# A state space mixer's elementwise work: Horner steps, compact products and rotations placed on VectorE

## The chip, the cores and the metric

The kernel runs on one core of a Trainium2 chip as one program. The metric is the time of one execution in device microseconds (us). TensorE multiplies matrices into PSUM, VectorE (DVE in the profile) and GpSimd (POOL) do elementwise work, ScalarE (ACT) copies and applies functions, SyncE (SP) issues the DMA transfers. GpSimd instructions here read and write SBUF only; VectorE reads and writes SBUF and PSUM.

## The reference

Two transformer blocks run one after the other on 512 tokens of width 1024. Only the first block's state space mixer bears on the change. For 32 groups of 16 channels with 64 complex states each it discretises a diagonal system, runs it over the sequence and mixes the result:

```python
h = rmsnorm(x, norm1_g[l]); hp = h @ w_in[l]
y_ssm = s5_mixer(hp[..., :512], ...)
y_nsa = nsa_mixer(hp[..., 512:1024], ...)
gate = sigmoid(hp[..., o4:])                   # 2 x 1024 columns
merged = gate0 * (y_ssm @ w_proj_ssm) + gate1 * (y_nsa @ w_proj_nsa)

def s5_mixer(u, a_re, a_im, log_dt, b_re, b_im, c_re, c_im, d_skip, w_glu, b_glu):
    dt = exp(log_dt)[:, None]
    mag = exp(a_re * dt)
    abar_re, abar_im = mag * cos(a_im * dt), mag * sin(a_im * dt)
    fr, fi = ((abar - 1) / (a_re + i a_im))     # real and imaginary part
    bbar = f * b                                # complex, 64 states x 16 channels
    bu = einsum('bsgc,gpc->bsgp', ug, bbar)
    x = associative_scan(x_t = abar * x_{t-1} + bu_t)
    y = einsum(x_re, c_re) - einsum(x_im, c_im) + d_skip * ug
    yg = gelu(y)
    return yg * sigmoid(yg @ w_glu + b_glu)
```

## The kernel before

A planner orders the instructions of each engine ahead of time from their dependencies and their place in the program; the chip then runs each engine's list in that order. Every float32 matrix product is split into a high and a low part, so a weight tile of 128x1024 is loaded (`wload`, line 217: a DMA to `raw`, a ScalarE copy to `wh`, a VectorE subtraction to `wl`) and takes 24 matmuls of 512 columns (`mm3`, line 204). Two `raw` buffers and three of `wh` and `wl` exist. In PSUM there are four buffers of the kind `mm`, three of the kind `aux` and one of the kind `sm`.

The first stage runs to about 208 us. `block1` (line 425) loads the parameters and calls `s5_params` (line 469), which works out the exponentials, sines and cosines by polynomials on tiles of 128x16, all on GpSimd (tile `s5s`). `s5` (line 553) projects the mixer's input (4 units of `win`, evicted to `uv`, spread by DMA to `ur`), then runs `s5_half` twice, once for each half of the states, with `gates` (line 1113) after each: 8 projection units whose results VectorE scales (`gt`, tt on line 189) and ScalarE passes through the sigmoid. At the end `glu` (line 763) projects the mixer's output. Only when the tiles of this stage are free can the attention stage (`nsa_proj`) allocate its own; its first instruction on GpSimd is the memset of `hsel` on line 790.

Inside `s5_half` time is cut into chunks of four steps. `cm` (line 605) multiplies complex parameter columns into the matrices of 128x8x32 by three VectorE instructions of 256 elements each: 8 calls build `T1` (tiles `s5A`, `s5B`) for the four lags and 8 build `CA` (`s5CAr`, `s5CAi`). Half of each 32-column block is zero, since two groups share a block. `P` (`s5Pr`, `s5Pi`) holds 128 powers of a phase, doubled in seven levels of six GpSimd instructions each. TensorE transposes `T1` to `W1` (line 657), builds the direct term `KT` and `G` (lines 666 to 685), and for each of two `jt` computes `wr`, `wi` in PSUM (line 694). VectorE turns them by the phase (four multiplications), GpSimd adds (`s5C` or `glus`), VectorE scans with decay `m4` (line 717, eight scans of 128), four multiplications turn the result back, GpSimd adds into `s5Xr`, `s5Xi`, and TensorE sums `py` (lines 733 and 735). `self.tt` on line 189 takes the engine as its last argument, so nearly all of this stands on lines 189, 194 and 195 of the profile.

Of the kernel before, what the change touches and what calls it, by code (L numbers as in the profile page):

```python
# [7 lines left out]
F32 = mybir.dt.float32  # L8
# [4 lines left out]
OP = mybir.AluOpType  # L13
# [9 lines left out]
C1 = 6.28125  # L23
C2 = 0.0019350051879882812
# [28 lines left out]
def pack(a):  # L53
    f = {}
# [35 lines left out]
    f["s5b"] = np.stack([bd(a["ssm_b_re"][0]), bd(a["ssm_b_im"][0])], 1)  # L90
# [87 lines left out]
class Kern:  # L178
# [246 lines left out]
    def block1(self):  # L425
# [5 lines left out]
        with ExitStack() as st0:  # L431
            mg = self.pool(st0, "mg")
            self.mg = mg
            self.y_ssm = [mg.tile([128, 4, T], F32R, name="ys" + n) for n in "HL"]
            with ExitStack() as st1:
                p = self.pool(st1, "s5c")
                prm = p.tile([128, 3, 16], F32, name="s5p")
                nc.sync.dma_start(prm, I["s5p"])
                par = self.s5_params(p, prm)
                xp = self.pool(st1, "s5h")  # L440
                xs, pre = [], []
                for k in range(4):
# [5 lines left out]
                self.s5(xp, p, hs, par, xs, pre)  # L448
# [20 lines left out]
    def s5_params(self, p, prm):  # L469

        nc, I = self.nc, self.I
        e = nc.gpsimd
# [4 lines left out]
        def new():  # L477
            cnt[0] += 1
            return big[:, cnt[0] - 1]

        def tt(a, b, op):
            o = new()
            self.tt(o, a, b, op, e)
            return o

        def ts(a, s1, op0, s2=None, op1=None):
            o = new()
            self.ts(o, a, s1, op0, s2, op1, e)
            return o

        add, sub, mul = OP.add, OP.subtract, OP.mult

        def exp_parts(x):

            x = ts(x, -87.0, OP.max, 88.0, OP.min)
            n = ts(x, 1.0 / math.log(2.0), mul, MAGIC, add)
            n = ts(n, MAGIC, sub)
            r = tt(x, ts(n, LN2_HI, mul), sub)
            r = tt(r, ts(n, LN2_LO, mul), sub)
# [5 lines left out]
            self.ts(si, n, 127.0, add, 8388608.0, mul, e)  # L505
            return q, si.bitcast(F32)

        q, s = exp_parts(ldt)
        dt = tt(tt(s, q, mul), s, add)
        q, s = exp_parts(tt(ar, dt, mul))  # L510
        em = tt(tt(s, q, mul), ts(s, 1.0, sub), add)
# [3 lines left out]
        r = tt(th, ts(k, C1, mul), sub)  # L515
        r = tt(r, ts(k, C2, mul), sub)
        r = tt(r, ts(k, C3, mul), sub)
        h = ts(r, 0.5, mul)
        h2 = tt(h, h, mul)
        s = ts(h2, -1.0 / (12 * 13), mul, 1.0, add)  # L520
        for i in (10, 8, 6, 4, 2):
            s = ts(tt(s, h2, mul), -1.0 / (i * (i + 1)), mul, 1.0, add)
        s = tt(s, h, mul)
        c = ts(h2, -1.0 / (13 * 14), mul, 1.0, add)
        for i in (11, 9, 7, 5, 3, 1):
            c = ts(tt(c, h2, mul), -1.0 / (i * (i + 1)), mul, 1.0, add)
        cm1 = ts(tt(s, s, mul), -2.0, mul)
        sn = ts(tt(s, c, mul), 2.0, mul)
        cs = ts(cm1, 1.0, add)
        nr = tt(tt(em, cs, mul), cm1, add)  # L530
        mag = ts(em, 1.0, add)
        a1r, a1i = tt(mag, cs, mul), tt(mag, sn, mul)
        den = tt(tt(ar, ar, mul), tt(ai, ai, mul), add)
        rd = new()
        nc.vector.reciprocal(rd, den)
        fr = tt(tt(tt(nr, ar, mul), tt(a1i, ai, mul), add), rd, mul)
        fi = tt(tt(tt(a1i, ar, mul), tt(nr, ai, mul), sub), rd, mul)

        def cmul(x, y):
            return (tt(tt(x[0], y[0], mul), tt(x[1], y[1], mul), sub),  # L540
                    tt(tt(x[0], y[1], mul), tt(x[1], y[0], mul), add))

        A = [None, (a1r, a1i)]
        A.append(cmul(A[1], A[1]))
        A.append(cmul(A[2], A[1]))
        A.append(cmul(A[2], A[2]))
        m2 = tt(mag, mag, mul)
        m4 = tt(m2, m2, mul)
        u2 = cmul((cs, sn), (cs, sn))
        u4 = cmul(u2, u2)  # L550
        return A, (fr, fi), m4, u4

    def s5(self, hp, p, hs, par, xs, pre):
        nc, I = self.nc, self.I
        A, F, m4, u4 = par
# [20 lines left out]
        self.proj(I["win"][0:4], hs, u_out, first=3, pre=dict(enumerate(pre)), mid0=norm, mid_at=-3)  # L576
        for a in range(2):
# [3 lines left out]
        self.s5_half(hp, 0, A, F, m4, u4, s5d, ur, uv1)  # L581
        self.gates(hs, 0)
        self.s5_half(hp, 1, A, F, m4, u4, s5d, ur, uv1)
# [3 lines left out]
    def s5_half(self, hp, hf, A, F, m4, u4, s5d, ura, uv1):  # L587
        nc, I = self.nc, self.I
        add, sub, mul = OP.add, OP.subtract, OP.mult
        e, ep = nc.vector, nc.gpsimd  # L590
# [34 lines left out]

# [4 lines left out]
        self.ts(P[0][:, :, 1], u4[0][:, ps], 1.0, mul, e=ep)  # L630
        self.ts(P[1][:, :, 1], u4[1][:, ps], 1.0, mul, e=ep)
        n = 1
        while n < 128:

            m = min(n, 127 - n)
            if m > 0:
# [9 lines left out]
                self.tt(t, xi, sr, mul, ep)  # L646
                self.tt(oi, xr, si, mul, ep)
                self.tt(oi, oi, t, add, ep)
            n *= 2

# [36 lines left out]
        for jt in (2 * hf, 2 * hf + 1):  # L687
# [11 lines left out]
            ab, cd = (t2("s5A"), t2("s5B")) if jt % 2 == 0 else (t2("s5W1r"), t2("s5W1i"))  # L699
            ta, tb, tc, td = ab[:, 0], ab[:, 1], cd[:, 0], cd[:, 1]  # L700
            if jt % 2 == 0:
                zc = t2("s5C")
                zr, zi = zc[:, 0], zc[:, 1]
            else:
                zr, zi = (tile([128, 512], "glus", 2) for _ in range(2))
# [1352 lines left out]
```

## Time and profile before

| what | value |
|---|---|
| median of 3 runs | 1677.97 us (1674.24 to 1678.4) |
| profiled execution | 1677.89 us, its span 1676.2 us |
| TensorE / VectorE busy in the span | 94% / 69% |
| ScalarE / GpSimd busy in the span | 44% / 30% |

A page of the profile gives each engine's busy time, the chain of work that ended last, and groups of instructions by line, engine and tile. Views of the trace used here are the busy time by stretch, the waits of one engine, the groups with shapes kept apart, and instructions in order of time. A group's mean is the duration of one instruction; neighbours on an engine overlap by a little, so the distance between two starts is what one costs in a sequence.

### The profile page before, as it was taken

The page shows a single profiled execution, that of the slowest core. Times are in us where ns is not written, and L with a number is a line of the kernel's source. Part 1 is how long each engine was busy: PE and PEld are TensorE (multiplying, and loading weights), DVE is VectorE, ACT ScalarE, POOL GpSimd, SP SyncE. Part 2 cuts the span into 40 slices and gives each one's busy share as a digit, 9 for nine tenths or more (in the row PEclk, how much of TensorE's full clock was granted, in tenths as well). Part 3 has the DMA queues.
Part 4 walks back from the last instruction along what each step waited for, and adds up shares of the span by engine and source line. Part 5 has one row for each costly group of instructions (what it writes and reads, how often), then busy time and mean ns, then how long its engine had stood idle before and what let it go on. Part 6 is the DMA issues. An engine that isn't in the chain of part 4 may idle for free.

```text
span 1676.2 us, 22389 instructions
## 1 busy us (share of the span) xinstructions
PE 1574.8 (94%) x8277; PEld 1311.6 (78%) x8277; DVE 1156.2 (69%) x2075; ACT 731.4 (44%) x1284; POOL 506.8 (30%) x586
## 2 busy tenths in 40 slices
PE   7779998899999999999999999989989899999997
PEld 5567776677798888888887888878878788888886
DVE  5889644576759963864446878576877798767655
ACT  4214725454444322342235555466654444434332
POOL 7866122221300000000022222224420466555552
PEclk9898999799999999999999999999999899999998
DMA  4231241001436773743221111111221223323322
GB/s 171 69 91 40 92 127 38 7 21 50 139 138 204 227 262 99 237 153 100 89 70 51 39 40 43 58 58 63 62 64 56 76 91 98 101 89 100 101 79 85
DMA packets 59756, 158.34 MB, mean 94 GB/s; under 512 B 12416, under 2 KB 19840, under 8 KB 59520
## 3 DMA queue, kind: packets, MB, share of 16 engines
q1 hardware_dynamic: 59648, 156.92, 29.4%
q8 instruction: 65, 1.06, 0.3%
q14 instruction: 43, 0.35, 0.1%
HBM read 152.57 MB, written 2.10 MB: 92 GB/s over the span
## 4 chain that ended last, share of the span: by engine, by line
PE 71%; DVE 15%; issue 4%; POOL 4%; ACT 4%; DMA 1%; SPq 0%; POOLq 0%; DVEq 0%; ACTq 0%
PE ps_mm L208 20%; PE ps_mm L210 20%; PE ps_mm L209 20%; DVE wl L189 2%; PE ps_sm L1093 2%; PE ps_mm L1082 1%; DVE caccm L198 1%; POOL s5s L189 1%; ACT L186 1%; DVE s5t L189 1%; DVE hgE L189 1%; POOL s5s L195 1%; DVE s5CAr L189 1%; PE ps_aux L1536 1%; DVE s5CAi L189 1%
## 5 line engine op out<-in xcount | busy, mean ns | idle before, releaser
L186 ACT ACTIVATE wh<-raw 128x1024 fp32r<-128x1024 f32 (+3 forms) x234 | 236.6, 1013 | 549.0 <-PE ps_mm L209 408.7
L189 DVE TENSOR_TENSOR wl<-raw,wh 128x1024 fp32r<-128x1024 f32 (+2 forms) x162 | 197.9, 1222 | 119.7 <-ACT wh L186 110.4
L198 DVE SCALAR_TENSOR_TENSOR caccf<-ps_mm,cwf,caccf 128x441 f32<-128x441 f32 (+2 forms) x308 | 206.7, 694 | 34.6 <-ACT ctapf L186 28.9
L189 POOL TENSOR_TENSOR wl<-raw,wh 128x1024 fp32r<-128x1024 f32 (+2 forms) x72 | 159.9, 2222 | 167.4 <-ACT wh L186 166.7
L208 PE MATMUL ps_mm<-h4H,wh 128*128 128x512 f32 (+1 forms) x368 | 137.1, 380 | 7.8 <-DVE caccf L198 7.6
L189 POOL TENSOR_TENSOR rr<-rv,nhalf 128x2 f32<-128x2 f32 x9 | 8.7, 969 | 435.9 <-DVE rv L195 435.9
L210 PE MATMUL ps_mm<-h4H,wl 128*128 128x512 f32 (+1 forms) x368 | 138.3, 378 | 0.0
L209 PE MATMUL ps_mm<-h4L,wh 128*128 128x512 f32 (+1 forms) x368 | 138.3, 379 | 0.0
L208 PE MATMUL ps_mm<-h2H,wh 128*128 128x512 f32 (+1 forms) x280 | 103.8, 372 | 0.0
L210 PE MATMUL ps_mm<-h2H,wl 128*128 128x512 f32 (+1 forms) x280 | 103.6, 371 | 0.0
L209 PE MATMUL ps_mm<-h2L,wh 128*128 128x512 f32 (+1 forms) x280 | 103.6, 371 | 0.0
L208 PE MATMUL ps_mm<-aH,wh 128*128 128x512 f32 (+1 forms) x272 | 102.6, 377 | 0.5 <-DVE x L189 0.5
L210 PE MATMUL ps_mm<-aH,wl 128*128 128x512 f32 (+1 forms) x272 | 102.7, 378 | 0.0
L209 PE MATMUL ps_mm<-aL,wh 128*128 128x512 f32 (+1 forms) x272 | 102.4, 377 | 0.0
L208 PE MATMUL ps_mm<-hH,wh 128*128 128x512 f32 x224 | 89.7, 407 | 11.3 <-ACT hH L186 10.7
L210 PE MATMUL ps_mm<-hH,wl 128*128 128x512 f32 x224 | 90.5, 406 | 7.7 <-DVE wl L189 7.7
L1228 DVE CUSTOM_DVE_ANT_0 msc<-wmod,cB,cols 128x1024 bf16<-128x1024 f32 x64 | 82.0, 1281 | 20.5 <-DMA wmod<-in_wmod 20.2
L209 PE MATMUL ps_mm<-hL,wh 128*128 128x512 f32 x224 | 90.9, 406 | 0.0
L208 PEld LDWEIGHTS ps_mm<-h4H,wh 128*128 128x128 f32 x368 | 68.7, 190 | 21.2 <-issue 7.7
L209 PEld LDWEIGHTS ps_mm<-h4L,wh 128*128 128x128 f32 x368 | 69.9, 190 | 13.2 <-DVE h4L L198 0.4
L210 PEld LDWEIGHTS ps_mm<-h4H,wl 128*128 128x128 f32 x368 | 69.8, 190 | 13.1
L208 PE MATMUL ps_mm<-faH,wh 128*128 128x512 f32 (+1 forms) x194 | 72.4, 373 | 0.0
(531 smaller groups left out, 4141.7 us busy)
## 6 DMA issues: line engine op xcount, KB each, us to landing
raw<-in_wup SPq DMA_DIRECT2D x76, 512.0 KB, 3.5
wmod<-in_wmod SPq DMA_DIRECT2D x48, 512.0 KB, 4.3
raw<-in_wdn SPq DMA_DIRECT2D x32, 512.0 KB, 3.5
raw<-in_win SPq DMA_DIRECT2D x28, 512.0 KB, 3.5
raw<-in_wout SPq DMA_DIRECT2D x8, 512.0 KB, 3.5
raw<-in_wdn2a SPq DMA_DIRECT2D x8, 512.0 KB, 3.4
raw<-in_wdn2b SPq DMA_DIRECT2D x8, 512.0 KB, 3.3
raw<-in_wdn2c SPq DMA_DIRECT2D x8, 384.0 KB, 3.1
```

The lines of the kernel that those rows point to most:

```text
L186: return self.nc.scalar.activation(o, i, f, **k)
L189: return (e or self.nc.vector).tensor_tensor(o, a, b, op)
L195: return e.tensor_scalar(o, a, s1, s2, op0, op1)
L198: return self.nc.vector.scalar_tensor_tensor(o, a, s, b, op0, op1)
L208: mm(ps, wh, xh, start=start, stop=False)
L209: mm(ps, wh, xl, start=False, stop=False)
L210: mm(ps, wl, xh, start=False, stop=stop)
L1082: nc.tensor.transpose(tp[:, 128 * b:128 * b + 128], P[g, i][:, 128 * b:128 * b + 128], self.ident)
L1093: nc.tensor.matmul(O[64 * g:64 * g + 64, 128 * i:128 * i + 128], self.V[:, b, c:c + 64], PT[g][:, 128 * b:128 * b + 128], start=br == 0 an ...
L1228: ins = nc.vector.tensor_tensor_reduce(sc, w, cB[:, c], 1.0, bm[:, m:m + 1], OP.mult, OP.add, acc)
L1536: nc.tensor.matmul(ps[:, j], EE[:, li, 128 * j:128 * j + 128], vw(EE[:, li])[:, j], start=True, stop=True)
```

## The change

`s5_params` is called after the mixer's projections in the program and not ahead of them, and all its instructions go to VectorE. Polynomials are evaluated by Horner steps of one `scalar_tensor_tensor` each, real and imaginary part are treated in one instruction where they can be. `cm` goes. `products` takes its place: `b` and `c` arrive without the zero half, ScalarE copies them to PSUM (`bc`, an `aux` tile held until both calls of `products` are done), and four lags are multiplied at once in instructions of 512 elements, one product in SBUF (`U`) and one in PSUM (`V`); two instructions on 64 partitions each combine them into zeroed tiles. The phase doubling and the additions of the rotations move from GpSimd to VectorE. The scans write to PSUM in place of `wr` and `wi`, which stay allocated until the second turn is done. GpSimd keeps the memsets and the additions for `KT`.

```diff
-                par = self.s5_params(p, prm)
-        big = p.tile([128, 144, 16], F32, name="s5s")
+        big = p.tile([128, 90, 16], F32, name="s5s")
+        def poly(x, cs):
+            q = ts(x, cs[-1], mul)
+            for c in cs[-2::-1]:
+                q = stt(q, c, x, add, mul)
+            return q
...
-            q = ts(r, 1.0 / 7.0, mul, 1.0, add)
-            for i in (6, 5, 4, 3, 2):
-                q = ts(tt(q, r, mul), 1.0 / i, mul, 1.0, add)
-            q = tt(q, r, mul)
+            q = poly(r, [1.0 / math.factorial(i) for i in range(1, 8)])
...
         self.proj(I["win"][0:4], hs, u_out, first=3, pre=dict(enumerate(pre)), mid0=norm, mid_at=-3)
+        par = self.s5_params(p, prm)
...
-        def cm(o, x, y, op):
-            t = tile([128, 8, 32], "s5t", 2)
-            pin(self.tt(t, y[1], bc(x[1]), mul, e))
-            pin(self.tt(o, y[0], bc(x[0]), mul, e))
-            pin(self.tt(o, o, t, op, e))
+        bcs = tile([128, 4, 8, 16], "s5b")
+        nc.sync.dma_start(bcs, I["s5bc"][:, :, ps])
+        bc = self.mmtile((128, 512), "aux").rearrange("p (n a c) -> p n a c", n=4, a=8)
+        self.act(bc, bcs)
+        def products(o, g, x, last):
+            gb = [g[:, c, ps, :, None].to_broadcast([128, 8, 4, 16]) for c in range(2)]
+            xb = [x[:, c, :, None, :].to_broadcast([128, 8, 4, 16]) for c in range(2)]
+            for c in range(2):
+                nc.gpsimd.memset(o[c], 0.0)
+                U = tile([128, 8, 4, 16], "s5t", 1)
+                V = self.mmtile((128, 512), "aux")
+                self.tt(U, gb[0], xb[c], mul)
+                self.tt(V.rearrange("p (a l c) -> p a l c", a=8, l=4), gb[1], xb[1 - c], mul)
+                for h in range(2):
+                    r = slice(64 * h, 64 * h + 64)
+                    d = o[c][r, :, :, 16 * h:16 * h + 16].rearrange("p a l c -> p (a l) c")
+                    u = U[r].rearrange("p a l c -> p (a l) c")
+                    v = V[r].rearrange("p (n c) -> p n c", c=16)
+                    last[c](d, u, v)
...
-                self.tt(t, xi, si, mul, ep)
-                self.tt(orr, xr, sr, mul, ep)
-                self.tt(orr, orr, t, sub, ep)
+                self.tt(t, xi, si, mul)
+                self.tt(orr, xr, sr, mul)
+                self.tt(orr, orr, t, sub)
...
-            self.tt(ta, wr, Pr, mul)
-            self.tt(tb, wi, Pi, mul)
-            self.tt(zr, ta, tb, add, nc.gpsimd)
-            self.tt(tc, wi, Pr, mul)
-            self.tt(td, wr, Pi, mul)
-            self.tt(zi, tc, td, sub, nc.gpsimd)
-            sr, si = ta, tc
-            for z, s in ((zr, sr), (zi, si)):
+            def turn():
+                self.tt(ta, wr, Pr, mul)
+                self.tt(wr, wr, Pi, mul)
+                self.tt(tc, wi, Pr, mul)
+                self.tt(wi, wi, Pi, mul)
+            turn()
+            self.tt(zr, ta, wi, add)
+            self.tt(zi, tc, wr, sub)
+            for z, s in ((zr, wr), (zi, wi)):
...
-            self.tt(tb, sr, Pr, mul)
-            self.tt(td, si, Pi, mul)
-            self.tt(X[0][:, :, 1:], v(tb), v(td), sub, nc.gpsimd)
-            self.tt(zr, sr, Pi, mul)
-            self.tt(zi, si, Pr, mul)
-            self.tt(X[1][:, :, 1:], v(zr), v(zi), add, nc.gpsimd)
+            turn()
+            self.tt(X[0][:, :, 1:], v(ta), v(wi), sub)
+            self.tt(X[1][:, :, 1:], v(tc), v(wr), add)
```

## Rows read from the trace of the kernel before

**Rows 1.** Busy time by stretch: length, busy us of each engine, clock, DMA.
```profile
0.00:40.00 40.00, 27.92 (x112) 21.94 (x113) 23.72 (x36) 19.96 (x27) 28.42 (x93) 1.00 0.50 176
40.00:49.00 9.00, 9.00 (x41) 7.47 (x40) 0.09 (x1) 2.34 (x2) 9.00 (x50) 1.00 0.20 51
49.00:109.50 60.50, 48.03 (x254) 39.59 (x253) 57.97 (x98) 12.19 (x20) 38.15 (x58) 0.89 0.28 82
109.50:129.30 19.80, 9.47 (x45) 8.17 (x43) 11.48 (x28) 2.70 (x4) 19.00 (x35) 0.74 0.22 70
...
174.83:208.60 33.77, 32.72 (x155) 26.70 (x154) 20.16 (x33) 25.93 (x42) 0.00 (x1) 1.00 0.29 93
```

**Rows 2.** TensorE's waits, 28 to 210 us: total us, times, longest.
```profile
PE ps_sm L735 <- POOL s5Xr L189: 10.3, 1, 10.3
PE ps_mm L210 <- DVE wl L189: 8.8, 3, 7.0
```

**Rows 3.** Chain that ended last, 40 to 210 us: start, us, what.
```profile
42.06 6.82 POOL s5s L189 x38
...
110.86 5.10 POOL s5Pr L189
...
172.63 2.20 POOL s5Xi L189
```

**Rows 4.** VectorE's groups, 0 to 210 us: count, busy us, mean ns, idle before.
```profile
L189 DVE TENSOR_TENSOR wl<-raw,wh 128x1024 fp32r<-128x1024 f32 x23 | 29.6, 1290 | 12.0 <-ACT wh L186 9.9 <-PE ps_mm L210 2.1
L189 DVE TENSOR_TENSOR s5t<-s5c,s5s 128x256 f32<-128x256 f32 x16 | 12.6, 804 | 0.0
L189 DVE TENSOR_TENSOR gt<-ps_mm,rbs 128x512 f32<-128x512 f32 x16 | 10.9, 680 | 0.9 <-PE ps_mm L210 0.9
...
L717 DVE TENSOR_TENSOR_SCAN s5A<-s5s,s5C 128x128 f32<-128x128 f32 x8 | 5.8, 788 | 0.0
...
L189 DVE TENSOR_TENSOR s5CAr<-s5c,s5s 128x256 f32<-128x256 f32 x8 | 5.6, 729 | 8.4 <-PE ps_sm L735 8.4
...
L717 DVE TENSOR_TENSOR_SCAN s5B<-s5s,s5C 128x128 f32<-128x128 f32 x8 | 2.7, 394 | 0.0
...
L189 DVE TENSOR_TENSOR s5t<-s5b,s5s 128x256 f32<-128x256 f32 x4 | 1.7, 419 | 9.0 <-POOL s5s L189 9.0
...
L189 DVE TENSOR_TENSOR s5B<-s5b,s5s 128x256 f32<-128x256 f32 x2 | 0.8, 414 | 0.0
```

**Rows 5.** VectorE in order of time, 72 to 92 us: start, us, what.
```profile
72.20 1.26 DVE L189 TENSOR_TENSOR s5CAr<-s5c,s5s 128x256 f32<-128x256 f32 x1
...
77.81 0.42 DVE L189 TENSOR_TENSOR s5t<-s5c,s5s 128x256 f32<-128x256 f32 x1
78.14 0.42 DVE L189 TENSOR_TENSOR s5CAr<-s5c,s5s 128x256 f32<-128x256 f32 x1
...
91.36 0.68 DVE L189 TENSOR_TENSOR s5W1r<-ps_aux,s5Pr 128x512 f32<-128x512 f32 x1
91.96 0.68 DVE L189 TENSOR_TENSOR s5W1r<-ps_aux,s5Pi 128x512 f32<-128x512 f32 x1
```

**Rows 6.** VectorE in order of time, 29 to 31 us: small dependent instructions.
```profile
29.87 0.16 DVE L189 TENSOR_TENSOR rt<-rt,rv 128x4 f32<-128x4 f32 x1
30.07 0.19 DVE L195 TENSOR_SCALAR rt<-rt 128x4 f32<-128x4 f32 x1
```

**Rows 7.** VectorE's groups, whole span: one that reads and writes PSUM.
```profile
L189 DVE TENSOR_TENSOR ps_aux<-ps_aux,caccf 128x512 f32<-128x512 f32 x22 | 15.3, 696 | 22.2 <-POOL caccf L189 22.2
```

**Rows 8.** Busy time by stretch, tile gt on VectorE alone: length, busy, clock, DMA.
```profile
0.00:174.83 174.83, 8.81 (x13) 0.91 0.29 92
```

**Rows 9.** TensorE in order of time, 109 us: matmuls of a gate unit.
```profile
109.25 0.40 PE L209 MATMUL ps_mm<-hL,wh 128*128 128x512 f32 x1
109.48 0.39 PE L210 MATMUL ps_mm<-hH,wl 128*128 128x512 f32 x1
```

**Rows 10.** GpSimd in order of time: the attention stage's first instruction.
```profile
208.67 0.16 POOL L790 MEMSET hsel<- 128x72 f32 x1 [33.84 <-issue]
```

More of the change, by code (lines that the diff above doesn't have):

```diff
@@ L88, in bd @@
         return o.reshape(128, 16, 32)
-    f["s5b"] = np.stack([bd(a["ssm_b_re"][0]), bd(a["ssm_b_im"][0])], 1)
+    gpc = lambda v: v.reshape(16, 2, 64, 16).transpose(1, 2, 0, 3).reshape(128, 16, 16)
+    f["s5bc"] = np.stack([gpc(a[k][0]) for k in ("ssm_b_re", "ssm_b_im")]
+                         + [gpc(a[k][0].transpose(0, 2, 1)) for k in ("ssm_c_re", "ssm_c_im")], 1)
     f["s5c"] = np.stack([bd(a["ssm_c_re"][0].transpose(0, 2, 1)), bd(a["ssm_c_im"][0].transpose(0, 2, 1))], 1)
@@ L514, in s5_params @@
         k = ts(k, MAGIC, sub)
-        r = tt(th, ts(k, C1, mul), sub)
-        r = tt(r, ts(k, C2, mul), sub)
-        r = tt(r, ts(k, C3, mul), sub)
+        r = stt(k, -C1, th, mul, add)
+        r = stt(k, -C2, r, mul, add)
+        r = stt(k, -C3, r, mul, add)
         h = ts(r, 0.5, mul)
         h2 = tt(h, h, mul)
[L520 to L530, printed above, removed]
-        mag = ts(em, 1.0, add)
[L532 to L546, printed above, removed]
+        s = poly(h2, [(-1.0) ** i / math.factorial(2 * i + 1) for i in range(1, 7)])
@@ new lines, in s5_params, with square @@
+        s = stt(s, 1.0, h, add, mul)
+        c = poly(h2, [(-1.0) ** i / math.factorial(2 * i) for i in range(1, 8)])
+        c = ts(c, 1.0, add)
+        cm1 = stt(s, -2.0, s, mul, mul)
+        u = new(2)
+        cs = ts(cm1, 1.0, add, o=u[:, 0])
+        sn = stt(s, 2.0, c, mul, mul, o=u[:, 1])
+        def square(x, o):
+            t = new(2)
+            self.tt(t, x, x, mul)
+            tt(t[:, 0], t[:, 1], sub, o=o[:, 0])
+            stt(x[:, 0], 2.0, x[:, 1], mul, mul, o=o[:, 1])
+            return o
@@ L547, in s5_params @@
+        u4 = square(square(u, new(2)), new(2))
+        x = tt(ar, dt, mul)
+        q, s = exp_parts(x)
+        em = tt(s, q, mul)
+        em = stt(s, -1.0, em, add, add)
+        mag = ts(em, 1.0, add)
         m2 = tt(mag, mag, mul)
         m4 = tt(m2, m2, mul)
[L549 to L553, printed above, removed]
+        A = p.tile([128, 2, 16, 5], F32, name="s5Ap")
+        Ad = lambda d: A[:, :, :, d]
@@ new lines, in s5_params @@
+        two = lambda v: v[:, None, :].to_broadcast([128, 2, 16])
+        self.tt(Ad(1), u, two(mag), mul)
+        n = new(2)
+        t = tt(em, cs, mul)
+        tt(t, cm1, add, o=n[:, 0])
+        tt(mag, sn, mul, o=n[:, 1])
+        t = tt(ar, ar, mul)
+        den = tt(ai, ai, mul)
+        tt(t, den, add, o=den)
+        nc.vector.reciprocal(den, den)
+        pr, pi, F = new(2), new(2), new(2)
+        self.tt(pr, n, two(ar), mul)
+        self.tt(pi, n, two(ai), mul)
+        tt(pr[:, 0], pi[:, 1], add, o=F[:, 0])
@@ new lines, in s5_params @@
+        tt(pr[:, 1], pi[:, 0], sub, o=F[:, 1])
+        self.tt(F, F, two(den), mul)
+        square(Ad(1), Ad(2))
+        square(Ad(2), Ad(4))
+        self.tt(pr, Ad(2), two(A[:, 0, :, 1]), mul)
+        self.tt(pi, Ad(2), two(A[:, 1, :, 1]), mul)
+        tt(pr[:, 0], pi[:, 1], sub, o=A[:, 0, :, 3])
+        tt(pr[:, 1], pi[:, 0], add, o=A[:, 1, :, 3])
+        G = p.tile([128, 2, 16, 4], F32, name="s5Gp")
+        nc.vector.tensor_copy(G[:, :, :, 3], F)
+        back = lambda c: G[:, c, :, 2::-1]
@@ L554, in s5 @@
+        Fb = lambda c: F[:, c, :, None].to_broadcast([128, 16, 3])
+        t = p.tile([128, 16, 3], F32, name="s5gt")
+        for c, op in ((0, sub), (1, add)):
+            self.tt(t, A[:, 1, :, 1:4], Fb(1 - c), mul)
+            self.tt(back(c), A[:, 0, :, 1:4], Fb(c), mul)
+            self.tt(back(c), back(c), t, op)
+        return A, G, m4, (u4[:, 0], u4[:, 1])
+    def s5(self, hp, p, hs, prm, xs, pre):
         nc, I = self.nc, self.I
-        A, F, m4, u4 = par
         s5d = p.tile([128, 16], F32, name="s5d")
@@ L627, in s5_half @@
+        T1 = [tile([128, 8, 4, 32], n) for n in ("s5A", "s5B")]
+        minus = lambda d, u, v: self.tt(d, u, v, sub)
+        products(T1, Gp, bc[:, 0:2], (minus, lambda d, u, v: self.tt(d, u, v, add)))
         P = [tile([128, 8, 128], n) for n in ("s5Pr", "s5Pi")]
@@ L641, in s5_half @@
                 t = tile([128, 8, 64], "s5pt")[:, :, :m]
[L642 to L644 removed]
+                self.tt(t, xi, si, mul)
+                self.tt(orr, xr, sr, mul)
+                self.tt(orr, orr, t, sub)
                 t = tile([128, 8, 64], "s5pt")[:, :, :m]
[L646 to L648 removed]
+                self.tt(t, xi, sr, mul)
+                self.tt(oi, xr, si, mul)
+                self.tt(oi, oi, t, add)
             n *= 2
+        nci = tile([128, 8, 32], "s5nci")
+        self.ts(nci, ci, -1.0, mul)
+        CA = [tile([128, 8, 4, 32], n) for n in ("s5CAr", "s5CAi")]
+        products(CA, A[:, :, :, 1:5], bc[:, 2:4], (minus, lambda d, u, v: self.stt(d, u, -1.0, v, mul, sub)))
         W1 = [tile([128, 8, 128], n) for n in ("s5W1r", "s5W1i")]
@@ L698, in s5_half @@
             t2 = lambda n: tile([128, 2, 512], n)
[L699 to L705, printed above, removed]
-            self.tt(ta, wr, Pr, mul)
-            self.tt(tb, wi, Pi, mul)
-            self.tt(zr, ta, tb, add, nc.gpsimd)
-            self.tt(tc, wi, Pr, mul)
-            self.tt(td, wr, Pi, mul)
-            self.tt(zi, tc, td, sub, nc.gpsimd)
-            sr, si = ta, tc
-            for z, s in ((zr, sr), (zi, si)):
+            ac = t2("s5A") if jt % 2 == 0 else t2("s5W1r")
+            zc = t2("s5C") if jt % 2 == 0 else t2("s5W1i")
+            ta, tc = ac[:, 0], ac[:, 1]
+            zr, zi = zc[:, 0], zc[:, 1]
+            def turn():
[7 more added lines that the diff above has]
+            for z, s in ((zr, wr), (zi, wi)):
                 for pl in range(4):
```

68 lines of the change are left out of this document (26 added, 42 removed).

## The prediction

> **What bounds the kernel now.** Only the first stage is touched, so I read its stretches first. From 174.83 us, where the last addition of the mixer ends on GpSimd [rows 3], to 208.6 us TensorE is busy for 32.72 of 33.77 us [rows 1], with three of the sixteen gate units (thirteen `gt` are done before [rows 8]), `glu` and the last output sums. The attention stage begins at 208.67 us [rows 10]. So the end of the stage is the time of the last X plus what TensorE still owes then. Before it TensorE is not full: 48.03 of 60.5 us in the stretch from 49, and 9.47 of 19.8 us from 109.5, there at a mean granted clock of 0.74 [rows 1]. TensorE's waits name the mixer: 10.3 us for X on GpSimd and 8.8 us for `wl` on VectorE [rows 2]. From 49 to 109.5 us VectorE is busy for 57.97 of 60.5 us [rows 1]: with the waits around it, it is what bounds this part.
>
> The chain of waits shows two kinds of loss. VectorE stands still: 9.0 us until GpSimd has the parameters, and 8.4 us while the second phase table and X are stuck on GpSimd [rows 4], where one instruction on 128x8 took 5.10 us [rows 3]. And both engines slow each other: the same VectorE multiplication of 256 elements takes 1.26 us at 72 us, beside GpSimd's doubling, and 0.42 us at 78 us, when GpSimd has stopped [rows 5]; the group means of 804 and 729 ns against 414 ns say that this is common [rows 4].
>
> **The change part by part**, along VectorE from 40 us to the last X (134.8 us before).
>
> *Idle time removed.* The parameters and X no longer come from GpSimd: -9.0 and -8.4 us [rows 4]. The last addition on GpSimd, 2.2 us [rows 3], goes too (its VectorE form is counted below).
>
> *Compact products.* 96 instructions of 256 elements go. Their fourteen groups in the two halves, from `s5t<-s5c` (12.6 us) to `s5B<-s5b` (0.8 us) [rows 4], add to 56.0 us busy; neighbours overlap by about 0.08 us (0.42 long, 0.33 apart [rows 5]), so 48 us of VectorE's time. In their place stand 4 calls of 8 instructions of 512 elements, 0.60 us apart [rows 5]: 19.2 us. Two of each four write 64 partitions, which I price alike. Net -28.8 us, most of it contention and not arithmetic. Writing PSUM costs no more: 696 ns for 512 elements read from and written to PSUM [rows 7], 0.68 us with PSUM read alone [rows 5].
>
> *Scans.* 32 scans, in four groups from `s5A` at 788 ns to `s5B` at 394 ns [rows 4]: busy 16.1 us, and at 394 ns 12.6 us. I count -3.5 us. Their new place in PSUM is priced at nothing by the row above; from 0.1 us less to 0.1 us more each the bounds are -3 and +3 us.
>
> *Phase doubling, added to VectorE.* 7 levels of 6 instructions, over 8, 16, 32, 64, 128, 256 and 504 elements. A small dependent instruction costs 0.20 us from start to start [rows 6], 256 elements 0.33, 512 elements 0.60 [rows 5]; 128 lie between, taken as 0.25. 6 x (4 x 0.20 + 0.25 + 0.33 + 0.60) + 0.4 for two copies = 12.3 us, twice 24.6 us. Nothing hides this on VectorE itself: other engines' work runs beside it.
>
> *Rotation additions, added.* 4 `jt` with 4 additions of 512 elements at 0.60 us: 9.6 us.
>
> *Parameters, added.* I count 95 instructions of 16 to 48 elements; at 0.20 us 19 us. VectorE is idle for 16.3 of the first 40 us [rows 1], but `s5p` and the projections come in pieces. Used gaps can be none (19 us stay behind 40 us) or nearly all (3 us stay); I take half of the idle time, 8 us, so 11 us stay. A cover that is gone costs the difference. What waits behind a parameter on VectorE's list is `wl` and `hL` of the mixer's own projection, by 0.2 us each.
>
> *Other moves.* The copies to PSUM are two more instructions on ScalarE, 12.19 busy of 60.5 us [rows 1]; the memsets fall to GpSimd, which has nothing else. On SyncE's queue one load of parameters replaces another of the same size. These I cost at nothing.
>
> Sum: -9.0 - 8.4 - 2.2 - 28.8 - 3.5 + 24.6 + 9.6 + 11 = -6.7 us. This leaves all other contention in. From the other side, with no gap: 40 + 11 (parameters) + 19.2 + 24.6 + 9.6 + 32 x 0.60 (multiplications) + 12.6 (scans) + 13 gate units at 1.29 + 0.60 [rows 4, 5] + 1.2 for two splits = 162.0 us, 12.8 us before 174.83. The second counts what VectorE has to do and the first what I could name; I take -11 us, nearer to the second, because the contention that is left in the first (`wl` at a mean of 1290 ns with the rest) has the same origin. With thirteen gate units done, the last X at 163.8 us and the same 33.8 us behind it, the stage ends at 197.6 us. The later stages are not touched. 1677.9 (the profiled execution, 1.7 us over its span, and the median to 0.1 us) - 11 = **1667 us**.
>
> [...] By the trace VectorE pays nothing for a PSUM partner [rows 5, 7]. [...]
>
> **The rivals.**
>
> *Gates done early* (faster than forecast). Each gate unit asks TensorE for 24 matmuls 0.23 us apart [rows 9], 5.5 us, and VectorE for 1.9 us [rows 4, 5]. If VectorE, no longer stalled, evicts all sixteen before the last X, X comes 5.7 us later and TensorE owes 16.5 us less: 3 x 3.6 = 10.8 us more gained, 1656 us. For: TensorE has 23 us of idle time in the two stretches [rows 1], and 10.3 us of it goes with one wait [rows 2]. Against: weights must come through two buffers.
>
> *VectorE starves the gates* (slower). Everything of the mixer stands before the gates in the program, and now 34 us more of it is on the engine that must also make `wl` and `gt`. If its planner's order holds gate units back, each unit late at the last X costs 5.5 - 1.9 = 3.6 us. It decides at three units: with ten of sixteen done at the last X the 11 us are used up, with nine or fewer the kernel is slower. With seven done: -11 + 6 x 3.6 = +10.6, 1688 us. For: TensorE has waited for `wl` up to 7.0 us at a time already [rows 2], and the doubling was not on VectorE then. Against: the new work is a chain of dependent instructions, between which the planner can put others.
>
> *The time goes into waits of VectorE* (no change). The parameters may stand wholly behind the projections (8 us more). And `wr`, `wi` now hold two of three `aux` buffers through both turns, so the next `jt` must wait for a buffer and then for eight matmuls, each no more than 0.23 us [rows 9]: 0 to 1.8 us, four times 0 to 7.4 us. Both together cancel the gain: 1678 us, at the worst 1682. The second half's table `P` needs the first half's free, so nothing can run ahead there; TensorE's gates can fill the gap, VectorE's evictions too.
>
> [...]
>
> **How the numbers follow.** Forecast 0.45 (1660 to 1674), gates early 0.20 (1656), waits 0.14 (1678), PSUM cost 0.06 (1673), starved gates 0.15 (1688). About 0.3%, 5 us, is what a measurement of this kernel can tell from no change. Faster by more: nearly all of the first two and most of the PSUM case, 0.69. Within: the waits, the edge of the forecast, 0.16. Slower: 0.15. The range is 1647 to 1684: below it lies gates early together with VectorE's gaps filled, above it half of the starved gates.
>
> **What would show each step.** `s5s` stands on VectorE with 0.2 us apart, done near 50 us; scans near 394 ns in all groups; no wait of TensorE for X of 10 us; VectorE over 95% busy from 50 us to the last X; that X near 164 us; `hsel` near 198 us. Wrong: fewer than eleven `gt` before the last X, `wl` waits of 7 us and more, or VectorE idle between the turns of two `jt`.

## The result and the profile after

The changed kernel takes 1655.84 us (median, 1655.67 to 1657.01), the kernel before 1676.99 (1674.24 to 1678.4) beside it: a ratio of 0.9878, 95% interval 0.9863 to 0.9892, so 21 us faster. The forecast was 11 us faster, 1667 us; the range, 1647 to 1684, holds the time, and the rival "gates done early" gave 1656. The profiled execution took 1655.87 us, its span is 1654.2, 22.0 below that of before.

The stretches of [rows 1] in the changed kernel, the end moved to its own last X (columns as there):

```profile
0.00:40.00 40.00, 28.41 (x102) 21.59 (x103) 33.97 (x147) 19.50 (x27) 5.36 (x14) 0.91 0.53 182
...
49.00:109.50 60.50, 60.50 (x342) 50.75 (x341) 55.57 (x111) 23.50 (x33) 8.92 (x15) 1.00 0.37 111
109.50:129.30 19.80, 19.80 (x130) 15.98 (x129) 18.38 (x44) 11.05 (x17) 3.08 (x4) 1.00 0.24 80
129.30:164.10 34.80, 30.54 (x148) 24.95 (x146) 27.74 (x54) 16.10 (x28) 0.21 (x2) 0.95 0.18 47
164.10:189.50 25.40, 17.77 (x71) 15.08 (x72) 13.38 (x23) 14.54 (x24) 0.00 (x0) 0.73 0.19 62
```

TensorE is full from 49 to 129.3 us, where it had 23 us of idle time before [rows 1]. After the last X it owes 17.77 us, not 32.72, but needs 25.4 us for them at a mean clock of 0.73. Busy time by stretch of tile `gt` on VectorE alone, as in [rows 8], and then the first instruction of the attention stage on GpSimd, as in [rows 10]:

```profile
0.00:164.10 164.10, 10.98 (x16) 0.97 0.34 107
```

```profile
189.54 0.16 POOL L827 MEMSET hsel<- 128x72 f32 x1 [40.40 <-DVE ysL L191]
```

All sixteen gate units are evicted before the last X, where it was thirteen. Of the 22.0 us, X gives 10.7 (174.83 to 164.10), the tail behind it 8.4 (33.8 to 25.4), and 2.9 lie behind the stage, which ends 19.1 us earlier. VectorE in order of time: parameters, small steps of the first half's doubling, first product, large steps, the two waits for `wr`, and the last X (start, us, what, idle time before it):

```profile
25.97 1.20 DVE L200 SCALAR_TENSOR_TENSOR s5s<-s5s 128x16 f32<-128x16 f32 x13
...
37.41 0.68 DVE L191 TENSOR_TENSOR s5t<-s5Gp,ps_aux 128x512 f32<-128x512 f32 x1
38.00 0.18 DVE L191 TENSOR_TENSOR s5pt<-s5Pi 128x16 f32<-128x16 f32 x1
38.09 0.18 DVE L191 TENSOR_TENSOR s5Pi<-s5Pr,s5Pi 128x16 f32<-128x16 f32 x1
...
59.26 0.68 DVE L191 TENSOR_TENSOR s5pt<-s5Pi 128x504 f32<-128x504 f32 x1
59.86 0.68 DVE L191 TENSOR_TENSOR s5Pi<-s5Pr,s5Pi 128x504 f32<-128x504 f32 x1
...
87.09 0.69 DVE L191 TENSOR_TENSOR s5W1r<-ps_aux,s5Pr 128x512 f32<-128x512 f32 x1 [2.23 <-PE ps_aux L733]
...
149.45 0.69 DVE L191 TENSOR_TENSOR s5W1r<-ps_aux,s5Pr 128x512 f32<-128x512 f32 x1 [4.11 <-PE ps_aux L733]
...
163.41 0.69 DVE L191 TENSOR_TENSOR s5Xr<-s5W1r,ps_aux 128x512 f32<-128x512 f32 x1
```

Its groups from 36 to 165 us, as [rows 4] (count, busy us, mean ns, idle time before and its releaser):

```profile
L191 DVE TENSOR_TENSOR ps_aux<-ps_aux,s5Pi 128x512 f32<-128x512 f32 x16 | 11.1, 691 | 0.0
...
L757 DVE TENSOR_TENSOR_SCAN ps_aux<-s5s,s5W1i 128x128 f32<-128x128 f32 x16 | 5.5, 413 | 0.0
L191 DVE TENSOR_TENSOR s5W1r<-ps_aux,s5Pr 128x512 f32<-128x512 f32 x8 | 5.5, 684 | 6.3 <-PE ps_aux L733 6.3
...
L191 DVE TENSOR_TENSOR ps_aux<-s5Gp,ps_aux 128x512 f32<-128x512 f32 x4 | 2.8, 693 | 0.0
```

The contention that [rows 4] show (804 and 729 ns for 256 elements, scans at 788) is gone from these groups: scans take 412 and 413 ns, products 0.69 us for 512 elements. A little is left elsewhere: three of the last doubling steps of the second half take 0.88 to 0.95 us, beside GpSimd's work on `KT`, where they took 0.68 in the first half. The chain of work that ended last, behind the last X (start, us, what), shows why the tail is not TensorE's work alone:

```profile
171.25 0.40 ACT yg L188
...
173.77 0.31 DVE uv L794
174.10 1.11 ACT yg L188
175.23 0.64 ACT ysH L188
...
178.41 0.43 PE ps_mm L211
...
182.21 0.23 PE ps_mm L211
```

Eight gelu pieces on ScalarE, eight copies on VectorE, a last gelu and a split come one after the other while TensorE waits for `ysH`, by TensorE's waits from 28 to 192 us (total us, times, longest):

```profile
PE ps_mm L210 <- ACT ysH L188: 7.5, 1, 7.5
```

Then its matmuls take 0.43 us each until 181 us, at a granted clock of 0.50 (178.2 to 181 us), and 0.23 after that, at 1.00 (181 to 189.5 us).

### The profile page after: what moved, and what is told of

It is laid out like the page before. It is cut to its first block, busy times and chain, and to the rows that moved or that the text cites. A ratio compares the mean times of both kernels' runs of the same rounds, so it can differ in the third digit from the quotient of the medians.

```text
span 1654.2 us, 22302 instructions
## 1 busy us (share of the span) xinstructions
PE 1571.7 (95%) x8277; PEld 1308.7 (79%) x8277; DVE 1155.2 (70%) x2209; ACT 733.0 (44%) x1286; POOL 399.6 (24%) x355
## 4 chain that ended last, share of the span: by engine, by line
PE 73%; DVE 10%; ACT 5%; issue 2%; POOL 1%; DMA 0%; POOLq 0%; DVEq 0%; ACTq 0%
PE ps_mm L210 21%; PE ps_mm L211 21%; PE ps_mm L212 21%; PE ps_sm L1130 2%; PE ps_mm L1119 1%; DVE caccm L200 1%; DVE wl L191 1%; ACT L188 1%; DVE hgE L191 1%; PE ps_aux L1573 1%; DVE caccf L200 1%; PE ps_aux L1097 1%; ACT wh L188 0%; PE ps_mm L1007 0%; DVE hgl L1486 0%
```

## The experiments

All medians are set against 1655.84 us; the kernel before, timed beside each, stayed between 1675.59 and 1676.99. "Stage end" is the first memset of `hsel`, "last X" the end of the last addition, "W1" the first copy by ScalarE of each half's transposed `T1`; these three are from one profiled execution, which for p_pool took 1661.23 us, 5.4 over its median, and for sbuf 1639.49, 3.1 under it. The medians rest on four executions each (before_p on ten), which scatter by 1 to 11 us. The planner orders every one of these kernels anew, so each difference holds its reordering too.

| run | median, us | ratio to before | stage end | last X | W1, two halves |
|---|---|---|---|---|---|
| changed kernel | 1655.84 | 0.9863 to 0.9892 | 189.5 | 164.1 | 51.8, 114.7 |
| par_pool | 1663.02 | 0.9905 to 0.9946 | 195.9 | 171.6 | 67.8, 129.5 |
| wide | 1662.21 | 0.9903 to 0.9938 | 192.9 | 168.3 | 48.7, 111.5 |
| p_pool | 1655.82 | 0.9843 to 0.9893 | 190.5 | 164.2 | 52.6, 114.8 |
| rot_pool | 1649.36 | 0.9820 to 0.9850 | 183.9 | 154.1 | 51.7, 111.2 |
| before_p | 1675.90 | 0.9987 to 1.0005 | 209.1 | 180.4 | 68.8, 131.6 |
| compact_only | 1663.82 | 0.9913 to 0.9944 | 198.7 | 164.0 | 67.3, 125.6 |
| both_pool | 1647.57 | 0.9813 to 0.9851 | 181.2 | 148.2 | 49.6, 112.0 |
| par_twice | 1662.54 | 0.9903 to 0.9936 | 194.6 | 167.7 | 62.1, 129.2 |
| rot_sbuf | 1649.80 | 0.9830 to 0.9860 | 183.6 | 152.7 | 52.0, 110.5 |
| v_sbuf | 1643.37 | 0.9777 to 0.9825 | 177.8 | 152.2 | 40.6, 104.9 |
| sbuf | 1642.61 | 0.9784 to 0.9828 | 176.5 | 146.5 | 44.1, 95.9 |
| sbuf_all | 1644.00 | 0.9787 to 0.9830 | 179.4 | 149.5 | 44.1, 96.6 |
| sbuf_hold | 1641.70 | 0.9776 to 0.9816 | 174.4 | 146.6 | 44.6, 101.7 |
| hold2 | 1655.07 | 0.9859 to 0.9892 | 186.5 | 154.5 | 54.3, 117.0 |
| v_mm | 1648.12 | 0.9824 to 0.9854 | 182.8 | 153.8 | 41.3, 106.1 |
| sbuf_p_pool | 1647.57 | 0.9810 to 0.9854 | 182.6 | 149.7 | 39.5, 98.6 |

**One part undone at a time.** First the parameters and the products:

```diff
 # par_pool: the old s5_params on GpSimd, called ahead of the projections
+                par = self.s5_params(p, prm)        # e = nc.gpsimd
 # wide: the old 96 instructions of 256 elements, on VectorE
-        products(T1, Gp, bc[:, 0:2], ...)
+        cm(B[0], F, (br, bi), sub) ...
```

> The changed kernel with one part undone: the parameters are worked out on GpSimd by the old polynomials, ahead of the projections in the program, and written into the same tiles. Theory A (the start of the mixer's chain counts): the products start near 52 us instead of 37 us, and since TensorE is full only from 49 us on, the stage ends 6 to 14 us later, near 1666 us. Theory B (TensorE, full from 49 to 129 us, is the bound, and the chain has slack): less than 3 us, near 1657 us.

> The changed kernel with one part undone: the 96 products of 256 elements, half of them zeros, in place of the 32 compact ones of 512, all with SBUF operands, GpSimd silent beside them. Theory A (VectorE's time on the way to X counts): 96 x 0.33 - 32 x 0.60 = 13 us more work on VectorE, of which at least half shows: 6 to 13 us slower than the changed kernel, 1662 to 1669 us. Theory B (most of what the products cost before was contention with GpSimd, and TensorE hides the rest): 0 to 4 us slower, near 1658 us.

7.2 and 6.4 us slower, as theory A of each. wide also holds no bank of `aux` for products; against v_sbuf below, which holds none for `V`, it is 18.8 us slower. With the parameters on GpSimd, VectorE stands still before the first product for 11.2 us and starts it at 50.34 us in place of 37.41. Next the phase doubling, then the rotations:

```diff
 # p_pool
-                self.tt(t, xi, si, mul)            # and the five others
+                self.tt(t, xi, si, mul, nc.gpsimd)
 # rot_pool: SBUF partners, wr and wi free after the first turn
+            self.tt(ta, wr, Pr, mul)
+            self.tt(tb, wi, Pi, mul)
+            self.tt(zr, ta, tb, add, nc.gpsimd)    # and the three others
```

> The changed kernel with one part undone: the phase doubling and its two copies run on GpSimd again. Theory A (what gained was that the mixer's chain no longer stands on GpSimd): the second half's table can start only when the first half's is free, near 96 us, and takes GpSimd some 26 to 35 us as in the kernel before, so X of the second half comes later and the kernel is 5 to 12 us slower than the changed one, near 1664 us. Theory B (VectorE's total work sets the stage): VectorE is relieved of some 18 us and the kernel is 3 us or more faster than the changed one, under 1653 us.

> The changed kernel with one part undone: the rotations with SBUF partners and their sixteen additions on GpSimd. Theory A (hand-overs between engines and sharing cost more than VectorE's 9.6 us): 2 to 6 us slower than the changed kernel. Theory B (VectorE's total work sets the stage): 2 to 6 us faster. In the chain, two hand-overs per jt with an addition of 1.3 to 1.8 us each should show in the trace either way.

Doubling on GpSimd makes no difference, which neither theory gave (these four executions scatter most, 1650.55 to 1661.23). The old rotations are 6.5 us faster, against theory A. Theory B has the sign, but VectorE's total work, its reason, is not enough: doubling on GpSimd takes more off VectorE (46.87 us busy of 60.5 from 49 us, for 55.57) and gains nothing. In the busy time by stretch of rot_pool the tail is nearly full:

```profile
154.00:164.10 10.10, 10.10 (x59) 8.78 (x58) 2.58 (x4) 9.63 (x19) 0.05 (x1) 1.00 0.12 28
164.10:175.00 10.90, 9.63 (x41) 7.05 (x40) 6.11 (x14) 7.65 (x13) 0.00 (x0) 1.00 0.14 48
175.00:183.90 8.90, 8.90 (x41) 7.37 (x40) 8.13 (x12) 6.63 (x11) 0.01 (x1) 1.00 0.51 177
```

X comes at 154.1 us, TensorE still has gate units then, and its clock stays at 1.00.

**One part alone.** The four undoings give back 7 of 21 us, so parts were also put on the kernel before:

```diff
 # before_p
-        e, ep = nc.vector, nc.gpsimd
+        e, ep = nc.vector, nc.vector
 # compact_only: products as changed; parameters, doubling, additions on GpSimd
 # both_pool: products and parameters as changed; doubling, additions on GpSimd
```

> The kernel before, with one thing of the change: the phase doubling is on VectorE. Theory A (which engine doubles the phases is indifferent, since what VectorE gains in undisturbed instructions it pays back in doubling): 1671 to 1681 us. Theory B (GpSimd's doubling is what slowed VectorE, which gets it back at once): 1664 to 1669 us, and the mean of the group s5W1i falls from 804 to near 400 ns. Theory C (the bound of VectorE decides, 57.97 of 60.5 us before, and 18 us are added): 1685 us and more.

> The kernel before with one thing of the change, the compact products: parameters, phase doubling and the additions of the rotations stay on GpSimd. Theory A (the products are worth what undoing them cost, 6.4 us): 1667 to 1673 us. Theory B (most of the 14 us that the single undoings leave unexplained come with the products, by less contention with the doubling): 1655 to 1664 us. Theory C (alone they gain nothing, since X waits for GpSimd anyway): 1674 us and more.

> The changed kernel with the phase doubling and the additions of the rotations both on GpSimd, and the rotations' partners in SBUF as before; parameters and compact products stay on VectorE. Each of the two alone on GpSimd gave 1656 (doubling) and 1649 us (additions). Theory A (GpSimd's list is what made the kernel before slow: X waits for the second half's doubling, as its 8.4 us of VectorE's idle time and TensorE's 10.3 us told): 1659 us and more. Theory B (the two don't meet once the parameters have left GpSimd): 1646 to 1653 us.

Doubling alone changes nothing, theory A, though the mechanism of theory B is there. In VectorE's groups of before_p the products are at their undisturbed price (804 ns before [rows 4]). The scans are nearer to it: the four groups add to 13.8 us where they had 16.1, `s5A` at 500 ns for 788, but `s5W1r`, beside GpSimd's additions, at 666 for 396. (`s5W1i`, which theory B puts at 804 ns before, stood at 660 and is at 399.)

```profile
L189 DVE TENSOR_TENSOR s5t<-s5c,s5s 128x256 f32<-128x256 f32 x16 | 6.3, 416 | 0.0
...
L717 DVE TENSOR_TENSOR_SCAN s5A<-s5s,s5C 128x128 f32<-128x128 f32 x8 | 3.5, 500 | 0.0
```

VectorE wins this back and spends it on doubling. compact_only gives 13.0 us (theory B, at its slow edge), both_pool 16.3 more, theory B again. VectorE's first product in order of time, for compact_only and then both_pool, shows what the parameters were worth:

```profile
51.69 0.69 DVE L191 TENSOR_TENSOR s5t<-s5Gp,ps_aux 128x512 f32<-128x512 f32 x1 [12.84 <-POOL s5Gp L191]
```

```profile
36.13 0.68 DVE L191 TENSOR_TENSOR s5t<-s5Gp,ps_aux 128x512 f32<-128x512 f32 x1
```

The first product is 15.6 us earlier and the last X 15.8. So the way from before to after is -13.0 for the products, -16.3 for the parameters, and +8.3 for doubling and rotations on VectorE with PSUM partners: these last two together cost time. The prices hold for this order only: taken off the changed kernel, the parameters' move is worth 7.2 and not 16.3 us.

**What costs in the rotations.** Engine or operand, one at a time, and the products' partner `V` likewise:

```diff
 # rot_sbuf: as rot_pool, additions on VectorE;  sbuf: this and
-                V = self.mmtile((128, 512), "aux")
+                V = tile([128, 512], "s5v")
 # v_sbuf: only this line;  sbuf_all: sbuf and
-        bc = self.mmtile((128, 512), "aux")...; self.act(bc, bcs)
+        bc = bcs
```

> The changed kernel, but the rotations take SBUF partners as before: the four multiplications of a turn write four SBUF tiles, and wr and wi are free after the first turn; their sixteen additions stay on VectorE. Theory A (the two PSUM banks held through both turns delay the next jt): it keeps the gain of the run that also moved the additions to GpSimd: 1647 to 1652 us, last X near 154 us, thirteen to fourteen gt before it. Theory B (the additions on VectorE are what costs; the banks don't matter): as the changed kernel, 1654 to 1658 us, last X near 164 us, sixteen gt before it.

> The one before in this list, and the second partner of the compact products is in SBUF too, not in PSUM. Theory A (a PSUM partner has no price of its own on VectorE, and none is saved where GpSimd is silent): the same time as with the partner in PSUM, within 3 us, products 0.60 us apart in both. [...] Theory C (two SBUF inputs are slowed by GpSimd's memsets and additions): products of 0.8 us and more, and 2 to 6 us slower.

> The changed kernel, with only the second partner of the compact products in SBUF; the rotations keep their PSUM partners. Beside the three others measured this completes a square (products x rotations). Theory A (each PSUM bank taken from aux costs time of its own: the products' banks delay the transposes that make W1 and so the first jt of each half): 1646 to 1651 us, about 7 below the changed kernel, and the first copies to W1 near 44 and 95 us in place of 52 and 115. Theory B (the banks that the rotations hold are the bound while they hold them): no difference, 1653 to 1657 us.

> Everything in SBUF, and the inputs of the compact products too: no copy to PSUM by ScalarE, so that the products take no aux bank at all, and most instructions of VectorE have two SBUF inputs. Theory A (banks): the same or faster than with that copy, 1637 to 1643 us, first copies to W1 at 44 us or earlier. Theory B (two SBUF inputs are slower, also beside a GpSimd with little to do): products of 0.75 us and more, 1645 to 1652 us.

rot_sbuf: theory A, as fast as with GpSimd's additions (1649.80 and 1649.36 us), so the engine is indifferent. sbuf is 7.2 us faster again, more than any of its theories gave, though `s5v` takes 680 ns where `ps_aux` took 693. v_sbuf: 12.5 us below the changed kernel, beyond theory A's range and with the rotations still in PSUM. So the two parts don't add: either helps, `V` by more. sbuf_all doesn't differ from sbuf, so the bank of `bc` costs nothing that shows. W1's copies say where: 44 and 96 us for sbuf, 52 and 115 in the changed kernel.

**Bank or place.** Three `aux` buffers serve `bc`, `V`, the transposes, `KT` and `wr`, `wi`, in the order of the program. Either `V` holds banks that the transposes need, or an operand in PSUM costs by itself. sbuf_hold and hold2 keep all operands in SBUF and take the bank; v_mm keeps `V` in PSUM and takes the bank elsewhere:

```diff
 # sbuf_hold                             # hold2
+   hold = self.mmtile(..., "aux")       # same
+   tensor_copy(hold[:, 0:1], s5d[:, 0:1])   # from V, once V is made
+   tensor_copy(hd, hold[:, 0:1])        # tt(hd, hold, last element of o[c])
 # v_mm
-                V = self.mmtile((128, 512), "aux")
+                V = self.mmtile((128, 512), "mm")
```

> Everything in SBUF (rotations and second product partner), but each product call also takes a PSUM bank that it doesn't need, from before its second partner is written until after its last instruction; one column is written and read, sixteen instructions of one column in all, some 1.5 us of VectorE. Theory A (the bank, and not where the operand lies, is what cost 7 us): 1647 to 1653 us, and the first copies to W1 at 51 us and later, as with the partner in PSUM. Theory B (the operand's place costs): 1641 to 1646 us.

> As the run that took a PSUM bank without need, but the bank is now really held: its one column is written from the second product partner after that is made, and read together with the last product written, so that it is taken from then to the end of the call; in the run before, nothing tied the two copies to the products, and they ran ahead. All operands stay in SBUF; sixteen small instructions, some 1.5 us. Theory A (three aux banks, held by the products, keep the transposes and so W1 and the first jt of each half back): 1647 to 1653 us, first copies to W1 at 51 us and later. Theory B (it is where the operand lies, or the order that follows from it): 1641 to 1646 us, first copies near 44 us.

> The changed kernel, with one thing: the second product partner takes its PSUM bank from the four of the projections (mm), not from the three of the mixer (aux). Theory A (the aux banks): 1642 to 1649 us, first copies to W1 near 44 us. Theory B (a PSUM partner costs VectorE wherever its bank comes from): 1653 to 1658 us, copies as in the changed kernel. Theory C (the gates need the fourth mm bank): 1659 us and more, with TensorE idle from 49 to 109.5 us.

sbuf_hold came out as theory B, but it tested nothing: its copies depend on no product, ran ahead of them (in the second half the last ended at 96.30 us, before the transposes were due) and held no bank when it mattered. hold2 ties them: 1655.07 us, 12.5 above sbuf and even beyond theory A's range, although `V` lies in SBUF. v_mm: theory A, 7.7 us below the changed kernel with `V` in PSUM. Theory C's sign is there too, TensorE busy for 52.94 of 60.5 us from 49, but the idle time is not the gates': all 7.56 us are one wait of the second half's transposes, in TensorE's order of time:

```profile
104.94 1.09 PE L696 MATMUL ps_aux<-ident,s5A 128*128 128x128 f32 x4 [7.56 <-DVE s5Pr L196]
```

They read `s5A`, done at 91.6 us, and not `s5Pr`; what VectorE finishes just before (104.11 to 104.79 us) is `s5Xi`, which reads a bank of the first half's turns. That this bank is what they waited for is a reading, not a test. The first copies to `s5W1r`, ScalarE in order of time, for the changed kernel, sbuf, hold2 and v_mm:

```profile
51.80 0.60 ACT L188 ACTIVATE s5W1r<-ps_aux 128x512 f32<-128x512 f32 x1 [1.37 <-PE ps_aux L696]
```

```profile
44.14 1.09 ACT L188 ACTIVATE s5W1r<-ps_aux 128x512 f32<-128x512 f32 x2 [2.28 <-PE ps_aux L696]
```

```profile
54.33 1.07 ACT L188 ACTIVATE s5W1r<-ps_aux 128x512 f32<-128x512 f32 x2
```

```profile
41.27 1.07 ACT L188 ACTIVATE s5W1r<-ps_aux 128x512 f32<-128x512 f32 x2
```

In the first half of these four runs the copy is late where a bank of `aux` is held, wherever the operand lies. The transposes that it copies show the same. In the changed kernel and then in both_pool, TensorE in order of time:

```profile
51.16 0.60 PE L696 MATMUL ps_aux<-ident,s5A 128*128 128x128 f32 x4
```

```profile
47.20 0.63 PE L696 MATMUL ps_aux<-ident,s5A 128*128 128x128 f32 x4 [0.47 <-DVE s5CAr L191]
```

In the changed kernel `s5A` is complete at 40.60 us, 10.6 us earlier; in v_mm the transposes follow it by 0.3 us (40.29). In both_pool they are seen to wait for `s5CAr`, which they don't read: it is the last reader of a `V`. With hold2 and v_mm that settles it for the bank. How a late copy turns into time at the end of the stage is not shown step by step: hold2 has its last X at 154.5 us, as early as v_mm, and its stage ends 3.7 us later. sbuf, 1642.6 us, is then the best understood of the fast versions (v_sbuf, one line, is within its scatter): TensorE is busy in all of 49 to 146.5 us and 27.02 of the 30.0 us behind, and what is left is its own work.

**Price of a small instruction.** The parameters worked out twice:

```diff
         par = self.s5_params(p, prm)
+        ... dt2 = prm, through par[2] ...
+        par = self.s5_params(p, dt2)
```

> The changed kernel, with the parameters worked out twice, one set after the other (the second from inputs that depend on the first): about 98 more instructions of 16 to 48 elements on VectorE. Theory A (each costs 0.085 us from start to start, as the first set did): the first product starts near 46 us in place of 37.4, and the time is 3 to 7 us longer (1659 to 1663), by the exchange seen when the parameters stood on GpSimd (first product 12.9 us later, 7.2 us longer). Theory B (0.20 us each, as the prediction priced them; the first set only hid in gaps): the first product near 57 us, 1666 us and more. Theory C (they hide behind the gates): no difference to 1656.

6.7 us longer, in theory A's range. The first product starts at 50.77 us, 13.4 later, where theory A had 46: 98 instructions at 0.085 us would be 8.3, and 3.9 are other work that the planner now puts between them (a `uv`, two `wl`, a `gt`). Most of the rest is a chain. VectorE in order of time, seven Horner steps of the exponential, each on the one before, and then fourteen in which the sine's and the cosine's can alternate:

```profile
37.54 1.43 DVE L200 SCALAR_TENSOR_TENSOR s5s<-s5s 128x16 f32<-128x16 f32 x7
...
43.02 1.27 DVE L200 SCALAR_TENSOR_TENSOR s5s<-s5s 128x16 f32<-128x16 f32 x14
```

That is 0.21 us from start to start for dependent ones and 0.085 for the others.

## Why the prediction came out too small

**The step that failed** is "with thirteen gate units done, the last X at 163.8 us and the same 33.8 us behind it". The last X came at 164.10, but sixteen units were done and 25.4 us lay behind it: 8.4 of the 11 us that the forecast is short of the profiled spans. The other 2.9 lie behind the stage. That X was right to 0.3 us is luck, as the terms of the sum show.

**Parameters, the largest term that was mis-sized.** The sum kept 11 us of them past 40 us, from 0.20 us each [rows 6]. But the first product starts at 37.41: thirteen small ones take 1.20 us, 0.085 from start to start. [rows 6] shows two instructions that depend on each other, and par_twice has 0.21 us for such a chain; where chains alternate or the planner puts other work between, it is 0.085. The prediction had the move at +2.0 us, 9.0 of idle time less and 11 of work more; compact_only against both_pool puts it at -16.3.

**Doubling**, 12.3 us a half from the same row, takes about 9.5: 6 x (0.085 + 0.085 + 0.11 + 0.145 + 0.20 + 0.335 + 0.60) + 0.17 by the starts, 5.5 us less in both halves. Products (0.60 apart) and scans (412 ns for 394) were sized right.

**The last X** was forecast at 163.8 and came at 164.10, by errors that cancel. From 162.0 without a gap: -11 for the parameters, -2.6 for the product that starts before 40, -5.5 for doubling, +5.7 for three more gate units (1.9 each), and +13.4 for VectorE's idle time from 49 to 164.1 us (4.9, 1.4 and 7.1 in the three stretches), which the forecast's last step had at some 1.8. That is 162.0; 2.1 us are not accounted for.

**Thirteen gate units** were carried over from the kernel before. VectorE had the time for sixteen, which the first rival said: 16.5 us less owed by TensorE would leave 17.3 of the 33.8 us, and 17.77 are left. It is not the parameters that decide this: par_pool, with its first product as late as the forecast had it, also has sixteen before its last X, as have wide, p_pool, before_p and par_twice. The rival's time, 1656, is right by errors that cancel: its X at 169.5 us is 5.4 too late, its tail of 17.3 us is 8.1 too short, since part of the 25.4 us is the dependent chain and TensorE's work at the lower clock (0.50), and 2.9 us lie behind the stage.

**Waits.** The rival of waits had the right mechanism, banks, at 0 to 7.4 us for `wr` and `wi`; rot_sbuf gives 6.0, and 6.3 us stand before VectorE's `s5W1r`, in two waits of 2.23 and 4.11 us where it allowed 1.8 each. So one of the prediction's own signs of being wrong, VectorE idle between the turns of two `jt`, came true, and VectorE was not busy for over 95% from 50 us to the last X but for 88% of 49 to 164.1. What the prediction nowhere asked is who else draws on `aux`: `V`, costed at nothing, cost more (12.5 us by v_sbuf). The starved gates didn't come: among TensorE's waits of this stage none for `wl` is left, where it was 8.8 us [rows 2].

**PSUM partners** cost VectorE next to no time of its own. With PSUM read and written an instruction takes 691 and 693 ns, with PSUM read alone 680 (`s5v` in sbuf), with SBUF alone 0.68 and 0.69 us (the first products of sbuf_all). The chances gave 0.06 to a PSUM cost, at 1673 us. No run shows the 6 us by which that lies above the forecast: 691, 693 and 680 ns are within 13 ns of each other. In its place the runs show a bank that others need: `V` in another bank of PSUM gives 7.7 us (v_mm), in SBUF 12.5 (v_sbuf).

**Behind the stage** the forecast left out 2.9 us of the profiled spans. They are within the scatter. From the start of the attention stage to the end of the span the eighteen profiled executions of this document, whose program is the same there, take 1461.3 to 1469.0 us, the kernel before 1467.5, the changed one 1464.7, and before_p, whose stage ends as late as before, 1464.5.

## What to carry to other kernels

Before an operand goes to PSUM, list every tile that shares its buffers and how long each is held: here intermediates in shared banks cost 13 us, with products of 693 ns against 680. Price small instructions by rows with independent work between them as well as by a dependent pair, and keep both as bounds. And when more work comes off the path, ask at what point the tail stops being the other engine's work and becomes a chain of latencies.

## What the runs showed of the hardware

With the partner in PSUM, GpSimd's doubling did not slow VectorE's products here. In p_pool `s5CAi` has a mean of 683 ns, in the changed kernel 681. The same two instructions `s5CAi` in order of time, with GpSimd doubling beside them: first the partner in PSUM (p_pool), then in SBUF (sbuf_p_pool, both halves):

```profile
51.38 1.38 DVE L200 SCALAR_TENSOR_TENSOR s5CAi<-s5t,ps_aux 64x512 f32<-64x512 f32 x2
```

```profile
49.14 2.36 DVE L200 SCALAR_TENSOR_TENSOR s5CAi<-s5t,s5v 64x512 f32<-64x512 f32 x2
...
109.22 3.19 DVE L200 SCALAR_TENSOR_TENSOR s5CAi<-s5t,s5v 64x512 f32<-64x512 f32 x2
```

GpSimd's own step beside `s5CAi`, in order of time, again p_pool and then sbuf_p_pool (there in the second half), takes 1.28 us with the partner in PSUM and 1.70 with it in SBUF:

```profile
50.94 1.28 POOL L191 TENSOR_TENSOR s5Pr<-s5Pr,s5pt 128x504 f32<-128x504 f32 x1
```

```profile
110.16 1.70 POOL L191 TENSOR_TENSOR s5Pr<-s5Pr,s5pt 128x504 f32<-128x504 f32 x1
```

So beside GpSimd's doubling the pair takes 2.36 and 3.19 us with both inputs in SBUF, against 1.38 with one of them in PSUM. The run itself:

> Rotations and second product partner in SBUF, and the phase doubling on GpSimd again. VectorE is busy for 59.87 of 60.5 us from 49 us without this. Theory A (what VectorE saves in doubling it pays back in slowed instructions, as in the kernel before): 1638 to 1647 us, products and turns beside GpSimd over 0.9 us. Theory B (GpSimd's chain is longer and the turns wait for it): 1648 to 1656 us. Theory C (VectorE is the bound): 1637 us or less.

1647.57 us, 5 above sbuf, between the ranges of theories A and B. The intervals of the two overlap, but the stage ends 6.1 us later: in the faster version the doubling's engine seems to matter again, with `s5CAi` at a mean of 1381 ns and a wait of 5.7 us of `s5CAr` for a memset queued behind the doubling. So the two halves of the change answer the same contention twice. With GpSimd nearly silent (8.65 of 60.5 us busy from 49 in sbuf, `s5CAi` at 684 ns) a PSUM partner protects from next to nothing and holds a bank.
